# The first u tiles of a hybrid decoder block: 256 tokens multiplied before their norm is known, the rest normalised in turned form

## The chip, the cores and the metric

The kernel runs on one core of a Trainium2 chip. Its metric is the device time of one execution in microseconds (us); lower is better. The engines are named as in the profile: PE is TensorE (products; PEld its weight loads), DVE is VectorE, ACT is ScalarE, POOL is GpSimd, SP is SyncE, which here only issues DMAs. L78 is line 78 of the kernel.

## The reference, cut to what matters

One decoder layer on 512 tokens of width 1024, with 16 meta tokens ahead of them. The start of it, which the change concerns:

```python
def rmsnorm(x, g):
    ms = mean(x * x, axis=-1)
    return x * rsqrt(ms + EPS) * g

h = rmsnorm(concat([meta_tokens, x]), g_mix_pre)      # 528 tokens x 1024
q, k, v, r, a, u, zg, zs = split(h @ w_in)            # 1024 x 6160
```

`a` (16 columns) goes through `w_gate_up` and a log-sigmoid, and its running sums are the decays of a gated linear attention over q, k, v. `u` (1024 columns) goes into S5, a diagonal complex recurrence of 64 groups with coefficients made from `a_re`, `a_im`, `log_step`, `b` and `c`. `zg` and `zs` are the sigmoid gates that merge the two. A squared-ReLU MLP of width 4096 follows. All of it is in float32.

## The kernel before, in words

**Products.** Every float32 operand of a large product is split into a high part (a copy in the rounded type float32r, made by ACT, `split_hi` L159) and a low part (the difference, made by DVE, `split_w_lo` L173). `mm3` (L186) adds three products for each of the 8 slices k of the contraction: high by high, high by low, low by high. So a tile of 128 output columns over 256 tokens is 24 matmuls. The 528 tokens (512 and the 16 meta tokens at the end) are taken in two halves, `HALVES` = 0 to 256 and 256 to 528. Weight tiles of 128 columns (512 KB) have three buffers each for the raw tile, its high and its low part. PSUM has four banks named `mm` and four named `sm`.

**The prologue** (L276 to L428) is in an order written out by hand: `InOrder` (L71) keeps DVE's and ACT's instructions in program order, and `pinned` does it for PE. SP loads the meta tokens, then x in four row tiles of 128 tokens with the first three u weight tiles between them. For each row tile, `squared` sums the squares on ACT, `rooted` makes 1/sqrt with one ACT and four small DVE instructions, `normed` multiplies on DVE by that column and by `gpre` (the gain `g_mix_pre`, spread over the partitions by two products with a row of ones), `turned` transposes eight blocks on PE, and `high` and `low` split the result into `xh` and `xl`. `busy` runs idle products on PE. u tiles 0, 1 and 2 do their first half in between; then come their second halves (L425 to L427), each followed by `u_out`, a store to DRAM issued by POOL. The 16 columns of `a` are split into `wa` (L421 to L423).

**After it** come `gate_weights` (L453), `low_rank` (L458, the product with `wa`), and a list of dense slots. `slot` (L500) first fetches weights for itself and `AHEAD` = 2 more (raw load on SP, high part on ACT, low part on DVE) and then runs the next product of the list: u tiles 3 to 7, four `zs` gates, gate `zg` 4 (L545 to L549). Here the scheduler orders each engine's instructions. Between the slots stand `gate_up` (L473), the S5 coefficients (`chain`, L623, a series of narrow DVE instructions that begins with the tile `ab`, loaded by POOL at L582), their powers, and `decay_sums` (L481): for each of four heads a subtraction and a running sum (`tensor_tensor_scan`) over 528 columns, in which `mask01` sets the sum to zero at each 128th column.

**Blocks.** The rest of the list (L1128 to L1138) is used up as filling for PE in the four heads of attention and the eight S5 blocks (loop at L1145): in each block `slot` is called five times between the pieces of the block. Among the slots are the gates `zg` 5, 6 and 7 (L1133).

Of the kernel before, what the change touches and what calls it, by code (L numbers as in the profile page):

```python
# [9 lines left out]
F32R = mybir.dt.float32r  # L10
# [6 lines left out]
P = 128  # L17
# [32 lines left out]
def hybrid_block(ctx: ExitStack, tc: tile.TileContext, io, out: bass.AP):  # L50
# [66 lines left out]
    S.activation(warm, warm, AF.Sqrt)  # L117
# [137 lines left out]
    def u_half(w, ut, q, within=None):  # L255

        a, b = HALVES[q]
        ps = bank("mm")
        feat_tile(w, xh, xl, a, b, ps[:, : b - a], within=within)

        def taken():
            src = ps.rearrange("p (c s) -> p s c", s=T8)
            first = NM // T8 + a // T8
            S.copy(ut[:, :, first : first + 32], src[:, :, :32])
            if q:
                S.copy(ut[:, :, : NM // T8], src[:, :, 32:34])

        return taken
# [9 lines left out]
    gpre = mk(pxt, [P, D], tag="gpre")  # L278
    grow = mk(pxt, [1, D], tag="grow")
    one_row = mk(pxt, [1, P], tag="one_row")  # L280
    V.memset(one_row, 1.0)
    nc.scalar.dma_start(grow, io["g_mix_pre"][0].rearrange("(o d) -> o d", o=1))
    xm = mk(pxt, [P, D], tag="xt", bufs=5)
    xts, raws = [], []
    loaded = nc.sync.dma_start(xm[:NM], io["meta_tokens"])
    ones = mk(pxt, [P, 256], tag="ones")
    V.memset(ones, 1.0)
    idle = bank()

    def busy(n):  # L290

        for _ in range(n):
            PE.matmul(idle[:, :256], ones[:, :P], ones, start=True, stop=True)
# [3 lines left out]

    def x_load(t):
        xt = mk(pxt, [P, D], tag="xt", bufs=5)
        xts.append((xt, P, t * P))  # L300
        return nc.sync.dma_start(xt, io["x"][0, t * P : (t + 1) * P, :])


    for kind, i in (("x", 0), ("x", 1), ("u", 0), ("x", 2), ("u", 1), ("x", 3), ("u", 2)):
        with behind():
            if kind == "x":
                loaded = x_load(i)
            else:
                loaded, raw = raw_w(w_in[:, C_U + i * P : C_U + (i + 1) * P])
                raws.append(raw)  # L310
    xts.append((xm, NM, SEQ))
# [3 lines left out]
    nc.gpsimd.dma_start(vecs, io["vecs"])  # L315
    V, S = InOrder(nc.vector), InOrder(nc.scalar)
    ss = mk(pxt, [P, 5], tag="xss")
    rs = mk(pxt, [P, 5], tag="xrs")
    xns = {}

    def squared(i):
        xt, n, _ = xts[i]
        sq = mk(pxt, [P, D], tag="xsq", bufs=1)
        S.activation(sq[:n], xt[:n], AF.Square, accum_out=ss[:n, i : i + 1])

    def rooted(i):

        n = xts[i][1]
        y, ssum = rs[:n, i : i + 1], ss[:n, i : i + 1]
        parts = mk(pxt, [n, 2], tag="xr_r", bufs=3)  # L330
        a, hm = parts[:, :1], parts[:, 1:]
        S.activation(a, ssum, AF.Sqrt, scale=1.0 / D, bias=epst[:n])
        yield
        V.tensor_scalar(hm, ssum, -0.5 / D, -0.5 * EPS, op0=ALU.mult, op1=ALU.add)
        V.reciprocal(y, a)
        V.scalar_tensor_tensor(a, y, hm, y, op0=ALU.mult, op1=ALU.mult)
        V.scalar_tensor_tensor(y, a, 1.5, y, op0=ALU.add, op1=ALU.mult)

    roots = {}

    def summed(i):
        squared(i)
        roots[i] = rooted(i)
        next(roots[i])

    def normed(i, cols=(0, 512)):
        xt, n, _ = xts[i]
        if i not in xns:
            xns[i] = mk(pxt, [P, D], tag="xn", bufs=3)
            next(roots[i], None)  # L350
        xn = xns[i]
        for c in cols:
            cc = slice(c, c + 512)
            V.scalar_tensor_tensor(xn[:n, cc], xt[:n, cc], rs[:n, i : i + 1], gpre[:n, cc], op0=ALU.mult, op1=ALU.mult)

    def turned(i, tag):
        return [turned_tokens(xns[i][: xts[i][1]], xts[i][1], q, tag if isinstance(tag, str) else tag[q]) for q in range(2)]

    def high(i, q, pvs):
        _, n, col = xts[i]  # L360
        split_hi(xh[:, 4 * q : 4 * q + 4, col : col + n], pvs[q])

    def low(i, q, pvs):
        _, n, col = xts[i]
        dst = slice(4 * q, 4 * q + 4)
        V.tensor_sub(xl[:, dst, col : col + n], pvs[q], f32(xh)[:, dst, col : col + n])

    gps = [bank() for _ in range(2)]
    for i, ps in enumerate(gps):
        PE.matmul(ps, one_row, grow[:, i * 512 : (i + 1) * 512], start=True, stop=True)  # L370
    busy(2)
    summed(4)
    V.tensor_copy(gpre[:, :512], gps[0])
    normed(4, (0,))
    summed(0)
    S.copy(gpre[:, 512:], gps[1])
    summed(1)
    normed(0)
    t0 = turned(0, "mm")
    busy(2)  # L380
    normed(1)
    hi0 = split_w_hi(raws[0])
    w0 = hi0, split_w_lo(raws[0], hi0)
    high(0, 0, t0)
    high(0, 1, t0)
    t1 = turned(1, "sm")
    high(1, 0, t1)
    high(1, 1, t1)
    for q in range(2):
        low(0, q, t0)  # L390
        low(1, q, t1)
    ut0, ut1, ut2 = (u_tile() for _ in range(3))
    take0 = u_half(w0, ut0, 0)
# [1164 lines left out]
```

## Time and profile before

| | |
|---|---|
| time, median of 3 runs | 884.01 us (882.16 to 884.28) |
| the profiled execution's own time | 883.62 us |
| its span, first to last instruction | 881.9 us |
| mean granted clock of PE | 0.997 |
| DMA | 177.36 MB, mean 201 GB/s |

The span is shorter than the execution's own time by 1.7 us. In the rows of the profile, busy times stand per engine with the number of instructions; "x8" is the number of instructions in a row; an idle time in square brackets names what the instruction had waited for. PE's instructions are pipelined, so a row lasts longer than the distance to the next one.

### The profile page before, as it was taken

The numbers are of one execution on the slowest core, as the hardware profiler recorded it, in microseconds if no ns is written. First come the engines' busy times: TensorE is split into PE (matmuls) and PEld (weight loads), VectorE is DVE, ScalarE is ACT, GpSimd is POOL, SyncE is SP. The second block draws the span as 40 slices with busy tenths as digits, with TensorE's granted clock in tenths as the row PEclk, the third lists the DMA queues.
The fourth block names the chain that finished last, engine by engine and source line by source line (L and its number), as shares of the span: only waits on it lengthen the run. The fifth ranks groups of instructions, "written<-read, shape, count | busy, mean of one in ns | idle before, by whom it ended". The sixth has DMA issues, their size and how long they took to land.

```text
span 881.9 us, 13276 instructions
## 1 busy us (share of the span) xinstructions
PE 869.5 (99%) x4856; PEld 742.5 (84%) x4856; DVE 648.6 (74%) x1148; ACT 437.7 (50%) x731; POOL 124.0 (14%) x224
## 2 busy tenths in 40 slices
PE   8999999999999999999999999999999999999996
PEld 6998989898988888888888888988888888888885
DVE  7989898868778698755445765576666678788886
ACT  6475466767655454434333543333222236665763
POOL 1223022030312213232000001021112100000001
PEclk9999999999999999999999999999999999999998
DMA  9647785555454857558545761589998966856564
GB/s 305 179 126 239 205 196 143 136 134 161 109 166 126 260 130 176 170 161 274 187 143 160 228 178 57 172 288 324 333 305 298 324 244 224 280 190 194 170 209 142
DMA packets 164988, 177.36 MB, mean 201 GB/s; under 512 B 18778, under 2 KB 125306, under 8 KB 164923
## 3 DMA queue, kind: packets, MB, share of 16 engines
q1 hardware_dynamic: 146056, 114.74, 44.8%
q0 software_dynamic: 17696, 57.84, 19.4%
q10 hardware_dynamic: 1170, 3.94, 1.3%
q8 instruction: 38, 0.62, 0.3%
q14 instruction: 28, 0.22, 0.1%
HBM read 141.06 MB, written 35.42 MB: 200 GB/s over the span
## 4 chain that ended last, share of the span: by engine, by line
PE 96%; DVE 2%; ACT 1%; DMA 0%; issue 0%; DVEq 0%; SPq 0%
PE mm L60 73%; PE sm L60 21%; PE sm L65 2%; DMA xt<-in_x_dram 0%; DVE xn L78 0%; DVE wlo L78 0%; ACT xsq L78 0%; DVE c L1483 0%; DVE xl L78 0%; PE mm L65 0%; DVE ede L604 0%; DVE c L1477 0%; ACT xh L78 0%; ACT whi L78 0%; DVEq L1554 0%
## 5 line engine op out<-in xcount | busy, mean ns | idle before, releaser
L160 ACT ACTIVATE whi<-wraw 128x1024 fp32r<-128x1024 f32 x101 | 107.0, 1059 | 236.1 <-PE mm L60 207.9
L175 DVE TENSOR_TENSOR wlo<-wraw,whi 128x1024 fp32r<-128x1024 f32 x101 | 123.4, 1222 | 106.7 <-ACT whi L160 106.5
L60 PE MATMUL mm<-xh,whi 128*128 128x512 f32 (+2 forms) x544 | 182.2, 335 | 0.5 <-ACT xh L78 0.5
L60 PE MATMUL mm<-xl,whi 128*128 128x512 f32 (+2 forms) x544 | 178.6, 328 | 1.1 <-DVE xl L78 1.1
L60 PE MATMUL mm<-xh,wlo 128*128 128x512 f32 (+2 forms) x544 | 178.9, 329 | 0.2 <-DVE wlo L78 0.2
L60 PEld LDWEIGHTS mm<-xh,whi 128*128 128x128 f32 x544 | 102.7, 189 | 10.6 <-issue 1.2
L60 PEld LDWEIGHTS mm<-xl,whi 128*128 128x128 f32 x544 | 102.8, 189 | 10.0 <-DVE xl L78 1.5
L60 PEld LDWEIGHTS mm<-xh,wlo 128*128 128x128 f32 x544 | 102.6, 189 | 9.7 <-DVE wlo L78 0.6
L60 PE MATMUL mm<-hh,whi 128*128 128x512 f32 (+1 forms) x280 | 104.0, 371 | 0.0
L60 PE MATMUL mm<-hl,whi 128*128 128x512 f32 (+1 forms) x280 | 103.8, 371 | 0.0
L60 PE MATMUL mm<-hh,wlo 128*128 128x512 f32 (+1 forms) x280 | 103.8, 371 | 0.0
L1420 DVE TENSOR_TENSOR wlo<-wraw,whi 128x1024 fp32r<-128x1024 f32 x56 | 68.4, 1222 | 20.2 <-ACT whi L1416 20.0
L60 PE MATMUL sm<-wlo,fh 128*128 128x512 f32 x192 | 74.8, 390 | 0.0
L60 PE MATMUL sm<-whi,fl 128*128 128x512 f32 x192 | 74.7, 389 | 0.0
L60 PE MATMUL sm<-whi,fh 128*128 128x512 f32 x192 | 74.7, 389 | 0.0
L1416 ACT ACTIVATE whi<-wraw 128x1024 fp32r<-128x1024 f32 x56 | 58.6, 1048 | 17.2 <-PE mm L60 11.7
L60 PEld LDWEIGHTS mm<-hl,whi 128*128 128x128 f32 x280 | 52.7, 188 | 9.1
L60 PEld LDWEIGHTS mm<-hh,whi 128*128 128x128 f32 x280 | 52.7, 188 | 9.1
L60 PEld LDWEIGHTS mm<-hh,wlo 128*128 128x128 f32 x280 | 52.7, 188 | 8.9
L160 ACT ACTIVATE fh<-f 128x512 fp32r<-128x512 f32 x48 | 30.3, 631 | 45.7 <-PE sm L60 30.6
L60 PE MATMUL mm<-gh,whi 128*128 128x512 f32 x128 | 49.8, 389 | 0.0
L60 PE MATMUL mm<-gl,whi 128*128 128x512 f32 x128 | 49.8, 389 | 0.0
(415 smaller groups left out, 1635.0 us busy)
## 6 DMA issues: line engine op xcount, KB each, us to landing
wraw<-in_w_ff_dram SPq DMA_DIRECT2D x56, 512.0 KB, 4.4
wraw<-in_w_in_dram SPq DMA_DIRECT2D x48, 512.0 KB, 4.1
w2raw<-in_w_ff_dram POOLq DMA_DIRECT2D x16, 1024.0 KB, 8.5
t2d<-w2t POOLq DMA_DIRECT2D x16, 1024.0 KB, 5.8
wraw<-t2d SPq DMA_DIRECT2D x32, 512.0 KB, 3.8
wraw<-in_w_glu_dram SPq DMA_DIRECT2D x16, 512.0 KB, 4.4
M<-kpad POOLq DMA_DIRECT2D x64, 64.0 KB, 2.6
wraw<-in_w_o_gla_dram SPq DMA_DIRECT2D x8, 512.0 KB, 7.9
```

The source lines that it names most:

```text
L60: ins = nc.tensor.matmul(*args, **kw)
L65: ins = nc.tensor.transpose(*args, **kw)
L160: S.activation(dst, src, AF.Copy, scale=scale)
L175: V.tensor_sub(lo, raw, f32(hi))
L1416: halved = S.activation(bh, raw, AF.Copy)
L1420: V.tensor_sub(bl, raw, f32(bh))
```

## The change

The parts, in the order of the program:

1. The input x is given also in turned form (features by tokens), as two arrays `x_cols0` (tokens 0 to 255) and `x_cols1` (256 to 527), and the gain as `g_cols`, one column for each k. These are made where the inputs are laid out, before the launch.
2. SP loads the turned first 256 tokens in four parts of two k; the first u weight tile comes in two halves from ACT's queue. Then SP loads w1, the rows of x 256 to 383, 384 to 511 and of the meta tokens, w2, the turned second half, w3, the rows 0 to 127 and 128 to 255, and w4. The rows are used for their squares alone.
3. For the first 256 tokens of u tiles 0 to 3, the product is made from g·x (`rh`, `rl`) without the per-token scale. The scale comes when the bank is emptied: DVE multiplies by a row that holds each token's 1/sqrt on all partitions (`raw_took`). That row is made by small products with a broadcast column (`spread`).
4. The second half is normalised in turned form (`normed(1)`: for each k one DVE instruction of 272 columns and one ACT copy, and a DVE difference for two k), and its products for tiles 0 to 2 run side by side, k by k.
5. Tile 3's raw product follows, with the squares and roots of rows 0 to 255 and their `spread` in its middle; then `normed(0)`, tile 3's second half, and both halves of tile 4 in the usual way. So five u tiles stand in the prologue, all written in fixed order, and the list of slots begins with u tile 5.
6. The transposes of x, the spreading of the gain and `xn` are gone. The split of `wa` comes at the end, behind the copies of tile 4.
7. The list of early slots has `zg` 4, 5 and 6 where it had `zg` 4, so 5 and 6 leave the later list, and two of the `slot` calls in the last block are left out.
8. `decay_sums` does the difference inside the scan, in five pieces for each head, without `mask01`. `c_rows` and the first fetches are held behind `wa`.

In the order of POOL's instructions, the load of `ab` (third in before) now stands behind the stores of u tiles 0 to 4 and the six loads of `wgu`.

The core of the diff:

```diff
+    def u_took(ps, ut, q, raw=False):
+        a = HALVES[q][0]
+        src = ps.rearrange("p (c s) -> p s c", s=T8)
+        first, n = NM // T8, 32
+        if raw:
+            V.tensor_mul(ut[:, :, first : first + n], src, scale_rows[0])
+            return
+        S.copy(ut[:, :, first + a // T8 : first + a // T8 + n], src[:, :, :n])
+        if q:
+            S.copy(ut[:, :, :first], src[:, :, n : n + first])
...
-    for kind, i in (("x", 0), ("x", 1), ("u", 0), ("x", 2), ("u", 1), ("x", 3), ("u", 2)):
+    for k in (0, 4):
+        first = nc.scalar.dma_start(raws[0][:, k : k + 4], w_in[k * P : (k + 4) * P, C_U : C_U + P].rearrange("(k p) n -> p k n", p=P))
+    for k in range(0, KT, 2):
+        with behind():
+            loaded = nc.sync.dma_start(xT[:, k : k + 2, :256], io["x_cols0"][:, k : k + 2])
...
+    for kind, i in (("u", 1), ("x", 2), ("x", 3), ("x", 4), ("u", 2), ("h", 0), ("h", 4), ("u", 3), ("x", 0), ("x", 1), ("u", 4)):
...
+    def taken_raw(k):
+        g = g8[:, k : k + 1]
+        S.activation(rh[:, k], xT[:, k, :256], AF.Copy, scale=g)
+        V.scalar_tensor_tensor(rl[:, k], xT[:, k, :256], g, f32(rh)[:, k], op0=ALU.mult, op1=ALU.subtract)
...
+    def spread(c, cols):
+        ps = bank()
+        for j, i in enumerate(range(c.start, c.stop)):
+            n = xts[i][1]
+            PE.matmul(ps[:, j * P : j * P + n], rs[:n, i : i + 1].to_broadcast([n, P]), ident[:n, :n], start=True, stop=True)
+        return ps[:, : cols.stop - cols.start]
...
+        def scaled(k):
+            V.scalar_tensor_tensor(xT[:, k, cols], xT[:, k, cols], g8[:, k : k + 1], rows[:, cols], op0=ALU.mult, op1=ALU.mult)
+            S.copy(xh[:, k, cols], xT[:, k, cols])
+        def rest(k):
+            kk = slice(k, k + 2)
+            V.tensor_sub(xl[:, kk, cols], xT[:, kk, cols], f32(xh)[:, kk, cols])
...
+    busy(5)
...
+    for k in range(0, KT, 2):
+        for i in range(2):
+            taken_raw(k + i)
+        split_part(w0, raws[0], slice(k, k + 2))
+    pair = bank("mm")
+    raw_product(0, w0, pair)
+    for k in (0, 4):
+        split_part(w1, raws[1], slice(k, k + 4))
+    raw_product(1, w1, pair)
+    for i in range(2, TT + 1):
         squared(i)
+    rooted(late)
+    w2_ = split_w(raws[2])
+    ps = spread(late, lasts)
+    S.copy(rows[:, lasts], ps)
+    pair2 = bank("mm")
+    raw_product(2, w2_, pair2)
+    normed(1)
+    seconds = [bank("mm"), bank("mm"), bank()]
+    c0, c1 = HALVES[1]
+    for k in range(KT):
+        for (hi, lo), ps in zip((w0, w1, w2_), seconds):
+            for i, (a, b) in enumerate(((hi, xh), (hi, xl), (lo, xh))):
+                PE.matmul(ps[:, : c1 - c0], a[:, k], b[:, k, c0:c1], start=(k == 0 and i == 0), stop=(k == KT - 1 and i == 2))
+    w3 = split_w(raws[3])
+    squared(0)
+    squared(1)
+    rooted(early)
...
+    raw_product(3, w3, pair2, within=(4, spread_early))
+    for i in range(3):
+        u_took(seconds[i], uts[i], 1)
+    for i in range(2):
+        raw_took(i, pair)
+        u_out(i, uts[i])
+    w4 = split_w(raws[4])
     normed(0)
+    raw_took(2, pair2)
+    u_out(2, uts[2])
+    uts.append(u_tile())
+    raw_took(3, pair2)
+    u_half(w3, uts[3], 1)
+    u_out(3, uts[3])
+    uts.append(u_tile())
+    for q in range(2):
+        u_half(w4, uts[4], q)
+    u_out(4, uts[4])
     wa = mk(pg, [P, KT, 32], F32R, tag="wa")
-    split_hi(wa[:, :, :16], wraw)
+    begun_s = S.activation(wa[:, :, :16], wraw, AF.Copy)
...
-            V.tensor_sub(mn[:, h], mn[:, h], ga[:, h])
             b2 = mk(pga, [P, NT], tag="b2", bufs=2)
-            V.tensor_tensor_scan(b2, mask01, mn[:, h], 0.0, op0=ALU.mult, op1=ALU.add)
+            for c in range(0, NT, P):
+                cc = slice(c, min(c + P, NT))
+                V.tensor_tensor_scan(b2[:, cc], mn[:, h, cc], ga[:, h, cc], 0.0, op0=ALU.add, op1=ALU.subtract)
...
-    for m in range(3, KT):
+    for m in range(5, KT):
         u_slot(m)
...
-    gate_slot(C_ZG, 4, zg, early_tile)
+    for m in range(4, 7):
+        gate_slot(C_ZG, m, zg, early_tile)
...
-        slot()
+        if b < NBLK - 1:
+            slot()
```

More of the change, by code (lines that the diff above doesn't have):

```diff
@@ L321, in squared @@
     def squared(i):
[L322 to L334, printed above, removed]
+        xt, n = xts[i]
@@ L356, in turned @@
[L356 to L370, printed above, removed]
@@ L412, in hybrid_block @@
-    t3 = turned(3, ("mm", "sm"))
-    take1()
-    for q in range(2):
-        high(4, q, t4)
-        low(4, q, t4)
-    for q in range(2):
-        high(3, q, t3)
-        low(3, q, t3)
-    take2()
+    def spread(c, cols):
[4 more added lines that the diff above has]
+        return ps[:, : cols.stop - cols.start]
@@ new lines, in hybrid_block, with split_part @@
+    w1 = tuple(mk(wp, [P, KT, P], F32R, tag=t, bufs=3) for t in ("whi", "wlo"))
+    def split_part(w, raw, kk):
+        split_hi(w[0][:, kk], raw[:, kk])
+        V.tensor_sub(w[1][:, kk], raw[:, kk], f32(w[0])[:, kk])
+    for k in range(0, KT, 2):
+        for i in range(2):
[6 more added lines that the diff above has]
+    raw_product(1, w1, pair)
@@ L1188, in hybrid_block @@
         next(following, None)
-        slot()
+        if b < NBLK - 1:
+            slot()
         if this:
```

163 lines of the change are left out of this document (66 added, 97 removed).

## The prediction

> **What bounds the kernel now.** I read the page first: its span, its busy shares and the chain that ended last.
>
> ```profile
> span 881.9 us, 13276 instructions
> ...
> PE 869.5 (99%) x4856; PEld 742.5 (84%) x4856; DVE 648.6 (74%) x1148; ACT 437.7 (50%) x731; POOL 124.0 (14%) x224
> ...
> PE 96%; DVE 2%; ACT 1%; DMA 0%; issue 0%; DVEq 0%; SPq 0%
> ```
>
> TensorE is busy 869.5 of 881.9 us, so at most 12.4 us can come from removing its waits. Next come the waits of TensorE.
>
> ```profile
> PE sm L60 <- DMA grow<-in_g_mix_pre_dram: 2.6, 1, 2.6
> PE mm L60 <- DVE xl L78: 1.1, 2, 0.7
> ```
>
> Both belong to the prologue (with three more rows of 0.5 us and less, they are all that the view lists). So I took the chain of waits of the first 60 us, and the windows.
>
> ```profile
> 1.26 4.25 DMA xt<-in_x_dram
> ...
> 27.71 18.86 PE mm L60 x151
> ```
>
> ```profile
> 0.00:28.00 28.00, 23.36 (x127) 18.06 (x128) 21.97 (x65) 19.49 (x37) 7.53 (x25) 1.00 0.93 292
> 28.00:40.00 12.00, 12.00 (x99) 11.52 (x99) 11.02 (x56) 4.97 (x11) 2.21 (x4) 1.00 0.50 140
> 40.00:60.00 20.00, 20.00 (x166) 19.91 (x165) 19.74 (x71) 12.46 (x27) 3.94 (x6) 1.00 0.51 131
> 60.00:80.00 20.00, 20.00 (x132) 18.41 (x131) 16.55 (x32) 14.47 (x25) 4.39 (x8) 1.00 0.61 197
> 80.00:100.00 20.00, 20.00 (x97) 16.88 (x96) 19.20 (x30) 8.09 (x12) 3.99 (x7) 1.00 0.82 241
> ```
>
> Columns: length, then busy time of PE, weight load, DVE, ACT, POOL. Two things carry the forecast. From 27.71 on TensorE never stops: 151 products in 18.86 us are 0.125 us each, 72 of them make the three second halves. And DVE is nearly as full in 28 to 100 (66.5 of 72 us), with only a little time before TensorE asks for its results.
>
> **The change, part one: the prologue.** My yardstick is the start L of the low-rank product, which stands behind the u tiles.
>
> ```profile
> 13.60 0.38 PE L60 MATMUL mm<-xh,whi 128*128 128x256 f32 x1 [0.25 <-ACT xh L78]
> ...
> 36.70 0.28 PE L60 MATMUL mm<-xh,wa 128*32 128x256 f32 x1
> ```
>
> In before L is 36.70 with three u tiles. The change has five there. One tile is 24×0.120 + 24×0.125 = 5.88 us, which before does later at full pace, so equal cost would be L = 36.70 + 2×5.88 = 48.46.
>
> The durations that I use:
>
> ```profile
> 5.53 1.06 ACT L78 ACTIVATE xsq<-xt 128x1024 f32<-128x1024 f32 x1 [1.15 <-DMA xt<-in_x_dram]
> 6.49 0.19 ACT L78 ACTIVATION_READ_ACCUMULATOR xsq<-xt 128x1 f32 x1
> 6.71 0.29 ACT L78 ACTIVATE xr_r<-xss,epst 128x1 f32<-128x1 f32 x1
> ...
> 8.76 1.04 ACT L78 ACTIVATE whi<-wraw 128x1024 fp32r<-128x1024 f32 x1
> ...
> 27.15 0.33 ACT L78 ACTIVATE wa<-waraw 128x128 fp32r<-128x128 f32 x1
> ```
>
> ```profile
> 7.69 1.41 DVE L78 SCALAR_TENSOR_TENSOR xn<-xt,xrs,gpre 128x512 f32<-128x512 f32 x2
> ...
> 19.66 1.22 DVE L78 TENSOR_TENSOR wlo<-wraw,whi 128x1024 fp32r<-128x1024 f32 x1
> ...
> 31.61 0.19 DVE L586 TENSOR_SCALAR eme<-emr 128x64 f32<-128x64 f32 x1
> 31.72 0.19 DVE L586 TENSOR_SCALAR emk<-emk 128x64 int32<-128x64 f32 x1
> ...
> 50.84 1.69 DVE L479 TENSOR_SCALAR mn<-sm,vecs 128x256 f32<-128x256 f32 x4
> 52.45 0.41 DVE L224 TENSOR_TENSOR lp4a<-lamp 128x256 f32<-128x256 f32 x1
> ...
> 67.83 0.71 DVE L485 TENSOR_TENSOR mn<-mn,ga 128x528 f32<-128x528 f32 x1 [1.30 <-ACT ga L483]
> ...
> 68.73 1.25 DVE L487 TENSOR_TENSOR_SCAN b<-mask,mn 128x528 f32<-128x528 f32 x1
> ```
>
> A DVE instruction starts some 0.07 to 0.08 us before the one ahead of it ends (0.19 long, 0.11 apart), so I charge 1.13 for 1024 columns, 0.65 for a normalising 512, 0.34 for 256. A normalising instruction of 256 or 272 columns, which before lacks, lies between 0.34 (the plain 256) and 0.65 (512); I take 0.40, near the lower row. A tile of squares with its sum costs 1.18 (5.53 to 6.71), a root 0.3, a high part 0.95 to 1.04.
>
> Up to 15.6 us. DVE makes the raw parts of the first tile in four groups of 2×0.40+0.34, 4.6 us, and TensorE follows it to about 9.6; the second raw tile ends near 13. That beats before, whose first product runs at 13.6. But then nothing can go on until the squares of x rows 256 to 511 and the meta tokens are summed. Ahead of and with these rows 3.21 MB are asked for (w0 0.52, turned x 1.05, w1 0.52, rows 1.11). How fast they come, in slices of 1.25 us of the first 50:
>
> ```profile
> GB/s 0 69 203 380 365 361 406 340 415 352 292 365 364 321 311 312 325 325 346 350 251 61 69 10 0 0 47 224 278 327 173 247 225 102 290 41 0 0 0 0
> ```
>
> The first nine slices hold 3.17 MB by 11.25 us. The first issue is now 0.4 us sooner, and in before x0 (0.58 MB with the meta tokens, crossed by 4.4) counted as landed at 5.51, 1.1 later: 12.0 us, between 10.9 (no such lag) and 13 (0.3 MB of other tiles mixed in). Then two squares to 14.4, the root 0.3, four small DVE operations 0.9: **15.6**. TensorE idles 2.6 us.
>
> 15.6 to 28.6. The weights of tile 2 are split behind the root (high 15.7, low 16.95), so raw 2 ends at 19.6. The 72 interleaved second halves take 9.0 us; normalising for them (8×0.41 + 4×0.6 = 5.8 us of DVE) runs ahead of them. The 40 transposes are gone; in before they stood in TensorE's gaps.
>
> 28.6 to L. Tile 3's weights take over tile 0's buffers, which the interleaving holds to its last k: high 27.9 to 28.95, low to 30.2, a stall of about 1.4. The squares of x0 and x1 stand behind that split on ACT (31.3), root and DVE to 32.4, the spreading product sits in the middle of raw 3 and waits another 1.0: raw 3 ends at 34.35, tile 3's second half at 37.35. DVE has the low part of w4 till 37.1 and then normalises the first 256 tokens, 8×0.40 + 4×0.6 = 5.5, to 42.6: tile 4's first half ends at 43.3 (stall 3.0), its second at 46.3. The split of `wa` now stands behind tile 4's last copies on ACT: some 0.5 for these, 0.33 and 0.28 for the two parts, with nothing else for TensorE: 47.4. The same bookkeeping over before's prologue gives 27.3 where the row says 27.71; I add that 0.4: **L = 47.8, a gain of 0.7** against 48.46 (bounds: 46.7 and 48.9 by the landing alone). So the early start is paid back by stalls at other places: 2.6, 1.4, 1.0, 3.0 and 1.1.
>
> **Part two: what the prologue now pushes back.** The S5 coefficients begin with `ab`. In before POOL issues its load third, at 2.95. In the changed order it stands on POOL behind the stores of tiles 0 to 4 and six `wgu` loads, and its store of tile 4 waits for that tile.
>
> ```profile
> 2.95 0.56 POOL L582 DMA_DIRECT2D ab<-in_a_step_dram  x1
> ...
> 25.98 1.94 POOL L449 DMA_DIRECT2D wgu<-in_w_gate_up_dram  x4
> ```
>
> ```profile
> wgu<-in_w_gate_up_dram POOLq DMA_DIRECT2D x6, 32.0 KB, 2.0
> ab<-in_a_step_dram POOLq DMA_DIRECT2D x1, 96.0 KB, 5.3
> ```
>
> Tile 4 is copied by 46.9; its store, four of the loads and `ab` itself, at 0.5 to 0.6 of issue each, make 50; landing 2.0 to 5.3 us after, with some waiting for the queue: **52 to 56, I take 54.5**, near the row of `ab` itself. From there DVE has, ahead of the low part of the ninth slot's weights (zg 5): 103 operations of 64 columns at 0.11 to 0.16 (15.0), 8 of 1024 (9.0), 10 of 512 (6.0), 20 of 128 and 256 (5.1), 20 pieces of scan (5.6; in before four scans of 1.17 and four differences of 0.63, 7.2), 8 gate rows of 0.41 (3.3), 1 for the rest: 45 us, so 99.5 (97 to 101). TensorE wants those weights at about 98.3 if nothing stopped it. **A new wait of 0 to 3 us, I take 1.2.** Behind this wlo on DVE stands the rest of the tables of block 0, and TensorE's only other need of them is this:
>
> ```profile
> 91.57 0.69 DVE L995 TENSOR_TENSOR M<-M,B 128x512 f32<-128x512 f32 x1
> ```
>
> ```profile
> 104.10 0.67 PE L60 MATMUL sm<-M,BA 128*32 128x128 f32 x16
> ```
>
> Before is 11.8 us early there; the change puts two gate slots (zg 5 and 6, 11.8 us) ahead of that product, and the tables end at 106 to 110 against a need at 115: no wait. Gate products 2 and 3 take banks that DVE empties in the same full stretch, 0.5 us.
>
> **Part three.** Two slots leave the last block, so TensorE's filling there is 11.8 us shorter and its tables come some 6 us ahead of use instead of 18: still ahead, cost nothing (4 us if they come 10 us later than I read). The turned copies of x are made before the launch, and 26 KB less of broadcast loads cost nothing, as SP's queue is not what ends.
>
> **Sum.** −0.7 + 0.5 + 1.2 = +1.0 on the profiled execution's 883.62 us (span 881.9 and 1.7 around it): 884.6. The median of the runs shown is 884.01, 0.4 above that execution, so this is less than 0.1% from it. A measurement of this kernel tells about 0.3%, 2.65 us, from no change: 881.4 to 886.7 counts as the same.
>
> **A rule that speaks to the start.**
>
> ```profile
> 10.31 1.91 PE L60 MATMUL sm<-ones 128*128 128x256 f32 x4
> ```
>
> ```profile
> 132.42 1.46 PE L60 MATMUL sm<-vtok,ktok 128*128 128x256 f32 x6
> ```
>
> The same records of 256 columns take 0.48 us at 10.3 and 0.24 at 132, though the granted clock reads 1.00 in both: early products run at half pace until about 12 us. Here that is hidden (raw 0 at 24×0.24 from 6 to 11.8, raw 1 after it at full pace to 14.8, still before 15.6). The Trainium skill, "TensorE: Matmul & The Clock Gate", Part 1, says that the clock starts at half and is released after about 3.4 us of sustained activity, and falls back after an idle window of the same length. The trace differs on the first half: nine microseconds after TensorE began it is still slow. The page's fall-back would make an idle stretch like the 2.6 us one costly if it grew to 3.4: some 1.7 us by the page's figure, an estimate.
>
> **The rivals.**
>
> *Sooner rows* (0.26): the rows land at 10.9 and the normalising instructions of 272 columns are as cheap as plain ones. Then L is 1.1 + 0.4 sooner, the 0.4 of my bookkeeping falls too, `ab` follows, and part two costs 0.5 at most or nothing: −0.7−1.5−0.4 = −2.6, 881.0. For it: GB/s in the early slices reached 415, and turned x comes in pieces of 1 KB. Against: before's own first tile was 1.1 late.
>
> *DVE backlog* (0.20), the other side: `ab` lands at 56 or later, DVE gets the 45 us done at 101 or later, and TensorE waits 3 to 4 us for the ninth slot, 887.4 with the 0.5. It decides from a landing at about 55.5. For it: DVE is 99% and 96% full at 40 to 60 and 80 to 100 even with an early start. Against: 1.6 us less scan work.
>
> *Clock* (0.06): TensorE falls back to half pace in the wait before 15.6 and stays there as long as at the start, 9.4 us with the work of 4.7: 889.3.
>
> *It does not do what it says* (0.04): the last block starves without its two slots, 4 us, 888.6; or tile 4 waits for DVE as long as the transposes did.
>
> **How the numbers follow.** The forecast has the remaining 0.44, between 882.5 and 886.3. Faster by over 0.3%: three quarters of the first rival and a small part of the forecast's lower end, 0.23. Slower: 0.15 of the second, the third and fourth, and 0.02 of the forecast, 0.27. The same: 0.50. The range must hold 8 in 10: it takes in the sooner rows with its own spread, 880.5, and the backlog to 888.0; beyond are the clock, half of the last and the tails.
>
> **What would show it.** A row of squares of x3 that starts near 12.0 (10.9 for the first rival); a spreading product at 15.6; waits of TensorE on `wlo` near 29 (1.4) and on `xl` near 40 (3.0); low-rank product at 47.8; the first operation on `ab` at 54.5; a wait on `wlo` of 1.2 near 98, and none on the M product. It is wrong if L is outside 46 to 49, or if a wait over 2 us stands at a place that I have not named.

## The result, and the profile after

The changed kernel takes 888.33 us (median of 5 runs, 887.17 to 890.96), the kernel before 882.68 us in the same comparison (5 runs, 882.03 to 884.28). The ratio is 1.0065, with a 95% interval from 1.0043 to 1.0087: **slower by 5.65 us**, where the forecast had +1.0 and a range that ended at 888.0. The profiled execution of after took 889.77 us, its span 887.8, 5.9 longer than before's 881.9.

The page of after, the rows that answer to those of before:

```profile
span 887.8 us, 13258 instructions
...
PE 866.4 (98%) x4824; PEld 740.9 (83%) x4824; DVE 648.4 (73%) x1169; ACT 438.9 (49%) x742; POOL 124.4 (14%) x220
...
PE 87%; DVE 6%; DMA 3%; ACT 2%; issue 1%; SPq 0%; DVEq 0%; ACTq 0%
```

TensorE has 3.1 us less to do (866.4 after 869.5) and yet the span is 5.9 longer, so 9 us of waiting are new. The chain that ended last says the same: 87% of it runs over TensorE, where it was 96%. The waits of TensorE in after (total, times, longest):

```profile
PE sm L60 <- DVE xrs L78: 2.6, 2, 2.1
PE sm L65 <- DVE e_gk L901: 2.2, 1, 2.2
PE mm L60 <- ACT whi L78: 2.0, 2, 1.7
PE mm L60 <- DVE xl L78: 1.8, 3, 1.0
PE mm L60 <- DVE wlo L174: 1.5, 1, 1.5
PE sm L60 <- DVE xss L328: 1.3, 1, 1.3
PE mm L60 <- DVE wa L78: 1.2, 1, 1.2
PE mm L60 <- DVE wlo L78: 0.8, 1, 0.8
PE mm L60 <- ACT xh L78: 0.4, 1, 0.4
```

The rows with L78 (and `xss`, at the very start) are the prologue, and most of them were forecast. Two stand behind it: `wlo` of L174, which was forecast, and `e_gk` of L901, which was not. Where they stand in time, with the start L of the low-rank product and the M product (timeline of TensorE):

```profile
16.80 1.00 PE L60 MATMUL sm<-ident,xrs 128*128 128x128 f32 x6 [2.12 <-DVE xrs L78]
...
50.43 0.28 PE L60 MATMUL mm<-xh,wa 128*32 128x256 f32 x1 [1.16 <-DVE wa L78]
...
102.22 0.50 PE L60 MATMUL mm<-xh,wlo 128*128 128x512 f32 x1 [1.50 <-DVE wlo L174]
...
118.78 0.66 PE L60 MATMUL sm<-M,BA 128*32 128x128 f32 x16
...
141.94 0.62 PE L65 MATMUL sm<-ident,e_gk 128*16 128x128 f32 x4 [2.18 <-DVE e_gk L901]
...
418.20 0.39 PE L60 MATMUL mm<-gh,whi 128*128 128x512 f32 x1
```

The answering rows of before, the last two of them in TensorE's timeline:

```profile
125.10 0.60 PE L65 MATMUL sm<-ident,e_gk 128*16 128x128 f32 x4
...
412.23 0.39 PE L60 MATMUL mm<-gh,whi 128*128 128x512 f32 x1
```

The last row is the first product of the GLU, behind all the u tiles and gates. There after is 5.97 late, and it is 5.9 late at the end; TensorE has no wait on record in between: **everything is lost by 142 us**, and the last blocks cost nothing. The loss is at three places. L stands at 50.43 against 48.46 for equal cost: 2.0. The waits at 102 and at 142 are 1.5 and 2.2. That is 5.7 of 5.97. This is the account of one execution, which at 889.77 us is 1.4 above the median.

### The profile page after: what moved, and what is told of

Same layout as the page of the kernel before. It is cut to its first block, busy times and chain, and to the rows that moved or that the text cites. A ratio compares the mean times of both kernels' runs of the same rounds, so it can differ in the third digit from the quotient of the medians.

```text
span 887.8 us, 13258 instructions
## 1 busy us (share of the span) xinstructions
PE 866.4 (98%) x4824; PEld 740.9 (83%) x4824; DVE 648.4 (73%) x1169; ACT 438.9 (49%) x742; POOL 124.4 (14%) x220
## 3 DMA queue, kind: packets, MB, share of 16 engines
q1 hardware_dynamic: 147448, 116.90, 45.7%
## 4 chain that ended last, share of the span: by engine, by line
PE 87%; DVE 6%; DMA 3%; ACT 2%; issue 1%; SPq 0%; DVEq 0%; ACTq 0%
PE mm L60 64%; PE sm L60 21%; PE sm L65 2%; DMA wraw<-in_w_in_dram 1%; DVE wlo L174 1%; DMA xt<-in_x_dram 1%; DVE b L512 1%; ACT xt L78 0%; DMA g<-in_g_cols_dram 0%; DVE xT L78 0%; SPq L1034 0%; DVE mta L234 0%; DVE epb L235 0%; DVE M L1012 0%; DVE c L1512 0%
## 5 line engine op out<-in xcount | busy, mean ns | idle before, releaser
L159 ACT ACTIVATE whi<-wraw 128x1024 fp32r<-128x1024 f32 x99 | 104.6, 1059 | 231.1 <-PE mm L60 200.2
L174 DVE TENSOR_TENSOR wlo<-wraw,whi 128x1024 fp32r<-128x1024 f32 x99 | 120.9, 1223 | 106.0 <-ACT whi L159 105.9
L60 PE MATMUL mm<-xh,whi 128*128 128x512 f32 (+2 forms) x504 | 170.5, 338 | 0.4 <-ACT xh L78 0.4
L60 PE MATMUL mm<-xl,whi 128*128 128x512 f32 (+2 forms) x504 | 167.4, 332 | 1.8 <-DVE xl L78 1.8
L60 PE MATMUL mm<-xh,wlo 128*128 128x512 f32 (+2 forms) x504 | 167.5, 332 | 1.5 <-DVE wlo L174 1.5
L60 PEld LDWEIGHTS mm<-xl,whi 128*128 128x128 f32 x504 | 95.2, 189 | 10.9 <-DVE xl L78 2.4
L60 PEld LDWEIGHTS mm<-xh,wlo 128*128 128x128 f32 x504 | 95.0, 189 | 11.0 <-DVE wlo L174 1.9
L60 PEld LDWEIGHTS mm<-xh,whi 128*128 128x128 f32 x504 | 95.1, 189 | 10.2 <-issue 1.0
L1449 DVE TENSOR_TENSOR wlo<-wraw,whi 128x1024 fp32r<-128x1024 f32 x56 | 68.4, 1223 | 20.7 <-ACT whi L1445 20.7
L1445 ACT ACTIVATE whi<-wraw 128x1024 fp32r<-128x1024 f32 x56 | 58.7, 1049 | 18.3 <-PE mm L60 11.7
```

Source lines behind the costliest of these rows:

```text
L60: ins = nc.tensor.matmul(*args, **kw)
L159: S.activation(dst, src, AF.Copy, scale=scale)
L174: V.tensor_sub(lo, raw, f32(hi))
L1445: halved = S.activation(bh, raw, AF.Copy)
L1449: V.tensor_sub(bl, raw, f32(bh))
```

## The experiments

My theory from these rows: (a) in the prologue the x rows land late, TensorE idles, its clock falls, and L is late; (b) the load of `ab` stands so late on POOL that VectorE carries its table work behind it up to 142 us, and TensorE waits for VectorE twice. The rivals were that the clock alone explains the prologue, that the new scans explain VectorE's lateness, and that TensorE's waits on VectorE would come anyway.

### The tables: earlier in the new kernel, later in the old one

**e1_ab_early**: the new kernel with the load of `ab` at its old place.

```diff
     nc.gpsimd.dma_start(vecs, io["vecs"])
+    ab = mk(p5, [P, 3, NST_N], tag="ab")
+    nc.gpsimd.dma_start(ab, io["a_step"])
...
-    ab = mk(q5, [P, 3, N], tag="ab")
-    nc.gpsimd.dma_start(ab, io["a_step"])
```

> The changed kernel, with the tile ab in a pool that exists before the prologue and its load issued right behind that of vecs, so that the S5 chain on DVE can begin behind the last eviction of tile 3 (about 46 us) and not at 56.5. Theory (DVE backlog): the waits of TensorE of 1.5 us at 102 and of 2.2 us at 142 both come from DVE's late start; both go, and the time falls from 888.3 by 3.0 to 3.9 us, to about 884.6. Rival (SP queue): the wait at 142 comes from the loads of the block's states, which stand behind weight loads on SP; then only the 1.5 goes, to about 886.8. Second rival (the waits belong to the moved slots): nothing changes, 888.

Measured: 890.27 us, ratio 1.0085 (1.007 to 1.01). No gain. TensorE's timeline has no wait at `e_gk` any more, but these:

```profile
51.90 0.39 PE L60 MATMUL mm<-xh,wa 128*32 128x256 f32 x1 [2.49 <-DVE wa L78]
...
99.86 0.50 PE L60 MATMUL mm<-xh,wlo 128*128 128x512 f32 x1 [1.72 <-DVE wlo L174]
...
142.65 0.60 PE L65 MATMUL sm<-ident,e_gk 128*16 128x128 f32 x4
```

With `ab` there, the scheduler puts the table steps ahead of the split of `wa` on VectorE. The wait at `wa` grows from 1.16 to 2.49, and the one on `wlo` stays (1.72): here the order that VectorE gets counted, and not the landing of `ab`. Behind the longer wait the granted clock is at 0.50 as well (window of 52 to 54 us). That the wait at `e_gk` is gone doesn't show that it hangs on the tables: VectorE has `e_gk` ready at 140.28, 1.6 sooner than in after (141.89), but TensorE comes to it 2.9 later (142.65, where after asked at 139.76). In e16 below, without this edit, it is ready at 139.82. So (b) is not shown by e1, and an earlier load doesn't repair the time.

**e4_before_ab_late**: the reverse. The kernel before, with that load held behind the last copy of the low-rank product.

```diff
             S.copy(alow[r0:r1, a:b], ps[:32])
+        S.copy(ab[:32, 0, :1], f32(alow)[:32, NT - 1 :])
+        nc.gpsimd.dma_start(ab, io["a_step"])
...
-    nc.gpsimd.dma_start(ab, io["a_step"])
```

> The kernel before, with one edit: the load of ab waits for the last copy of the low-rank product (about 44 us), so that the S5 chain on DVE begins near 48 us, 11 us behind the start of the low-rank product (in the changed kernel 6 us behind it). Theory (DVE backlog): it alone makes the kernel before slower, 4 to 9 us, with waits of TensorE on DVE (low parts of weights, or the M product at 104) where it has none now. Rival: DVE makes the time good within its 11.8 us of slack, and the time stays within 1 us of 882.7.

Measured: 895.6 us, ratio 1.0141 (1.0124 to 1.0158), 12.7 us lost with nothing else changed. Its timeline of TensorE, and a window of it (length, busy time of PE, weight load, DVE, ACT, POOL, granted clock):

```profile
108.43 0.58 PE L60 MATMUL mm<-xh,wlo 128*128 128x256 f32 x1 [9.79 <-DVE wlo L175]
```

```profile
108.00:114.00 6.00, 5.57 (x28) 5.57 (x29) 6.00 (x11) 0.53 (x2) 0.00 (x0) 0.57 0.38 103
```

One wait of 9.79, and then a granted clock of 0.57 on average for 6 us. Late tables alone can cost far more than the whole change does.

**e5_chain_in_gap**: `ab` early, and the first three of the table steps in the fixed order, right behind the normalising of the second half.

```diff
     normed(1)
+    for _ in range(3):
+        next(steps)
     seconds = [bank("mm"), bank("mm"), bank()]
```

> The changed kernel, with the load of ab early and the first three steps of the S5 chain (47 narrow DVE instructions, about 6 us) written into the prologue's fixed order behind the second normalisation, where DVE idles from 24.2 to 31.8 us. Theory (DVE backlog by amount of work): the low-rank product still starts near 50.4 (not at 51.9 as with the early load alone, which put chain instructions ahead of the split of wa), and TensorE's waits on DVE near 102 (1.5) and 142 (2.2) both go: about 884.6. Rival (place in the queue): the low part of the ninth slot's weights waits because the scheduler puts table work ahead of it on DVE, however much has been done before; then 1.5 to 1.7 us stay near 100, and the time is about 886.2.

Measured: 890.98 us, ratio 1.009 (1.0075 to 1.0105). Both late waits are gone, and one has come in the prologue, on the low part of u tile 3's weights, which stands behind the steps:

```profile
37.17 0.58 PE L60 MATMUL mm<-rh,wlo 128*128 128x256 f32 x1 [4.84 <-DVE wlo L78]
```

L goes to 56.16, 5.7 later than in after. That is more than the two late waits together (3.7), so they would be gone by TensorE's own lateness, whatever the tables do. And `e_gk` is ready at 141.77, against 141.89 in after: with the steps done early it is no sooner. So e5 doesn't show (b) either. What it shows is that this place in the prologue does not hold the steps for nothing.

### The clock

**e2_fill** puts five idle products behind the second raw tile; **e3_both** is this together with e1; **e15_fill_both** has the five and three more at the start. **e16_after_again** is the changed kernel once more, in the same comparison as e15.

```diff
     raw_product(1, w1, pair)
+    idle = bank()
+    busy(5)
```

> The changed kernel, with five more idle products on TensorE behind the second raw tile, so that it does not idle between 14.7 and 16.8 us. Theory (clock): the granted clock of 0.50 between 18 and 21.5 us follows from that idle stretch; with it filled the clock stays at 1.00, raw tile 2 takes 2.9 us and not 4.6, the low-rank product starts about 1.5 us sooner (48.9) and the time falls by about 1.5, to 886.8. Rival (the low clock comes from something else, such as the way the first 20 us are loaded): the clock falls all the same, and the time stays at 888.3 or rises by what the idle products delay.

> Both edits, the early load of ab and the five idle products. If the two causes are separate, the gains add: 888.3 - 3.7 - 1.5 = 883.1, which is about the kernel before (882.7). If the 1.5 us at the start are given back as a longer wait later, it is the same as the early load alone, about 884.6.

> The changed kernel with eight idle products at the start instead of five, and five behind the second raw tile. Theory (clock): neither half-clock stretch (8 to 11 and 18 to 21.5 us) is left, the low-rank product starts 1.5 to 2 us sooner than in the changed kernel run beside it, and the median is lower by 1 to 2. Rival (what the start gains, the waits on DVE near 100 and 142 take back): the median is the same within 0.7.

> The changed kernel again, unaltered, beside the two others: 888.3, between 887 and 891 in single executions.

Measured: e2 888.81 (1.0066, 1.0051 to 1.0081), e3 888.55 (1.0069, 1.0046 to 1.0092), e15 888.58 (1.0065, 1.0052 to 1.0077), e16 889.51 (1.0079, 1.0064 to 1.0093). The windows of after show what the filling was for. The first two are stretches of 2 us, the last three stretches of 3.41 us:

```profile
19.00:21.00 2.00, 2.00 (x11) 2.00 (x11) 2.00 (x6) 1.46 (x4) 0.00 (x0) 0.50 1.02 401
21.00:23.00 2.00, 2.00 (x17) 2.00 (x16) 2.00 (x6) 1.29 (x4) 0.00 (x0) 0.87 1.23 290
```

```profile
4.38:7.79 3.41, 1.68 (x8) 1.01 (x7) 1.69 (x5) 2.16 (x6) 0.00 (x0) 1.00 1.04 332
14.62:18.03 3.41, 1.29 (x9) 1.11 (x8) 2.02 (x6) 2.34 (x5) 0.00 (x0) 1.00 1.12 370
31.68:35.09 3.41, 2.03 (x13) 1.63 (x13) 2.05 (x6) 2.44 (x6) 0.00 (x0) 1.00 0.20 45
```

The granted clock is 0.50 at 19 to 21; the products of raw 2 then follow one another at 0.21 us instead of 0.12. The half clock lasts from 18.1 to 21.5 and costs raw 2 about 1.5 us; an earlier stretch is at 7.9 to 11.3. In the 3.41 us ahead of them TensorE was busy for 1.68 and 1.29; the third stretch (2.03) has no fall behind it. That is no sharp limit: in e16, e7 and e2 a fall came behind 1.87, 1.94 and 2.22 of 3.41.

In e2 the fall at 18 is absent (one at 9.3 is there) and L is 49.45, a gain of 1.0 in the trace. But the median of e2 is that of after. The second execution of after, e16, helps to see why. Its timeline of TensorE, and that of e15 behind it:

```profile
49.05 0.27 PE L60 MATMUL mm<-xh,wa 128*32 128x256 f32 x1 [1.16 <-DVE wa L78]
...
100.85 0.50 PE L60 MATMUL mm<-xh,wlo 128*128 128x512 f32 x1 [1.50 <-DVE wlo L174]
...
139.88 0.62 PE L65 MATMUL sm<-ident,e_gk 128*16 128x128 f32 x4 [1.51 <-DVE e_gk L901]
```

```profile
49.05 0.28 PE L60 MATMUL mm<-xh,wa 128*32 128x256 f32 x1 [1.16 <-DVE wa L78]
...
101.78 0.50 PE L60 MATMUL mm<-xh,wlo 128*128 128x512 f32 x1 [2.44 <-DVE wlo L174]
...
139.84 0.62 PE L65 MATMUL sm<-ident,e_gk 128*16 128x128 f32 x4 [0.50 <-DVE e_gk L903]
```

e16 is the same program as after, with the clock at half from 9.4 to 12.8 and not at 18: the fall depends on the execution, and L is 1.4 sooner without the one at 18 (49.05 against 50.43). e15 has no half clock at all and no earlier L than e16. And the two waits behind L are together 2.94 in e15 and 3.01 in e16; VectorE has `e_gk` ready at 139.8 in both. So what TensorE gained at the first wait it lost at the second.

How much of the 5.65 can be the clock? The granted clock of each execution is on record. Of the ten executions of the changed kernel (after and e16) the three with 0.996 or 0.997 take 887.2 to 888.6 us, the three with 0.991 take 890.6 to 891.0. So the clock goes with some 3 us between one execution and the next, but those with the highest clock are still 4.5 to 5.8 above the kernel before. And e7, below, has both falls in its profiled execution (at 8.5 and 18.7) and nevertheless the time of before. So the clock adds to single executions and is not the cause of most of the 5.65.

### The rows

**e7_rows_early** loads x rows 0 and 1 ahead of u tile 3's weights, so that their squares, root and spreading run during the interleaved second halves. With this the order of the work changes as well: the spreading stands inside those products, and the first half is normalised in two parts, one on each side of the split of tile 3's weights.

```diff
-    for kind, i in (("u", 1), ("x", 2), ("x", 3), ("x", 4), ("u", 2), ("h", 0), ("h", 4), ("u", 3), ("x", 0), ("x", 1), ("u", 4)):
+    for kind, i in (("u", 1), ("x", 2), ("x", 3), ("x", 4), ("u", 2), ("h", 0), ("h", 4), ("x", 0), ("x", 1), ("u", 3), ("u", 4)):
...
+        if k == 5:
+            spread_early()
...
+    normed(0, 0, 4)
+    w3 = split_w(raws[3])
+    normed(0, 4)
+    raw_product(3, w3, pair2)
```

> The changed kernel, with the rows of x 0 to 255 loaded ahead of w3, their squares, roots and spreading product during the interleaved second halves, and half of the first half's normalisation ahead of the low part of w3, the other half right behind it. DVE and ACT idle there (24 to 31). TensorE's waits between 31 and 45 us (3.8 in all: 0.3, 0.8, 0.5, 0.4, 1.0, 0.4, 0.4) should shrink to about 1, and the low-rank product start near 47.5 instead of 50.4. If TensorE's later waits on DVE keep their size: 885.4. If DVE's backlog takes it back (the chain starts no earlier in the same degree): 887 to 888.

Measured: 882.64 us (10 runs, 881.15 to 885.64), ratio 0.9996 (0.9986 to 1.0006): all of the loss is gone. TensorE's timeline:

```profile
46.31 0.28 PE L60 MATMUL mm<-xh,wa 128*32 128x256 f32 x1 [1.16 <-DVE wa L78]
...
97.80 0.50 PE L60 MATMUL mm<-xh,wlo 128*128 128x512 f32 x1 [1.19 <-DVE wlo L174]
...
135.15 0.60 PE L65 MATMUL sm<-ident,e_gk 128*16 128x128 f32 x4
...
411.40 0.39 PE L60 MATMUL mm<-gh,whi 128*128 128x512 f32 x1
```

L is 4.1 sooner than in after, the `e_gk` wait is gone, and the end is 6.8 sooner (span 881.0). The stalls at the spreading of the first rows and at tile 4 do not stand in its list of waits. `ab` is used first at 51.9, 4.6 sooner. VectorE has `e_gk` ready at 134.51, 7.4 sooner than in after, and TensorE asks for it 4.6 sooner. So the order of the prologue sets both parts of the loss: the late L and the waits behind it. Which of the three changes of e7 does how much is not shown, nor is the way by which they reach `e_gk`; that it goes through the place of `ab` behind tile 4's store is argued only.

**e6_wa_early** moves the split of `wa` ahead of tile 4's products.

```diff
     u_out(3, uts[3])
+    wa = mk(pg, [P, KT, 32], F32R, tag="wa")
+    begun_s = S.activation(wa[:, :, :16], wraw, AF.Copy)
+    begun = V.tensor_sub(wa[:, :, 16:], wraw, f32(wa)[:, :, :16])
     uts.append(u_tile())
```

> The changed kernel, with the split of wa ahead of tile 4's product in the fixed order instead of behind its last copies. The forecast's term of 1.1 us (1.2 in the trace of the changed kernel) goes, the low-rank product starts at 49.2: 887.1. Rival: DVE's later waits take it back, since the rest of DVE's work is no earlier: 888.3.

Measured: 890.07 us, ratio 1.0081 (1.0064 to 1.0097). The wait of 1.16 is gone and L is 48.02 in its trace, but the gate products now wait for the banks that VectorE empties (0.70 and 0.97 near 66), `wlo` 1.49 near 102, `e_gk` 0.98. Against e16, which lacks the edit, L is 1.0 sooner and these waits are together 1.1 longer: the gain of TensorE ahead of a late VectorE is handed on as a wait.

### The scans

**e11_scan_back** is the new kernel with before's subtraction and masked scan; **e13_before_scan** is the kernel before with the new pieces.

```diff
-            V.tensor_sub(mn[:, h], mn[:, h], ga[:, h])
-            V.tensor_tensor_scan(b2, mask01, mn[:, h], 0.0, op0=ALU.mult, op1=ALU.add)
+            for c in range(0, NT, P):
+                cc = slice(c, min(c + P, NT))
+                V.tensor_tensor_scan(b2[:, cc], mn[:, h, cc], ga[:, h, cc], 0.0, op0=ALU.add, op1=ALU.subtract)
```

> The changed kernel with the running sums of the kernel before (four differences, four scans of 528 columns with the mask). DVE has about 1.6 us more work by the durations of the kernel before. Theory (backlog by amount): TensorE's waits on DVE near 102 and 142 grow by about as much in all, 1 to 1.6 us: 889.5. Rival (the waits come from the place in the queue, not from the amount): no change, 888.3.

> The kernel before with the changed running sums alone (20 pieces, no differences). DVE has some 1.6 us less work at 68 to 82 us, where TensorE waits for nothing: no change, 882.9 to 883.3. Rival (a shorter DVE queue is worth time even here): 1 us faster.

Measured: e11 896.84 (1.016, 1.0146 to 1.0174); e13 886.14 (1.0034, 1.0022 to 1.0046). In e11 the old scans bring not 1.6 but 8.5 us over after. The 1.6 of work can't be the reason alone. VectorE's timeline, and below it TensorE's:

```profile
114.93 1.22 DVE L790 TENSOR_TENSOR M<-M,prm 128x1024 f32<-128x1024 f32 x1 [6.62 <-DMA M<-in_b_cols_dram]
```

```profile
148.15 1.02 PE L65 MATMUL sm<-ident,e_gk 128*16 128x128 f32 x4 [3.65 <-DVE e_gk L904]
```

With the other scans VectorE got another order. In it an instruction that needs a DMA stands 6.62 us at the head of the queue, with two low parts of weights behind it, and TensorE waits 0.84, 2.53 and 3.65, which is 3.3 more than in after. Most of the rest is the clock: it falls to 0.50 for two stretches of 3.4 us from 120.3 on and for one from 147.7 on, beside the two early ones that after has too, and each costs up to 1.7 us. e13's own profiled execution (884.07) has waits of only 0.32, 0.39 and 0.24 near 87, 98 and 108 beyond those of before. That explains some 0.5 to 1 of its 3.26 us, and the rest stays open: the profiled execution is the fastest of five. So the rival of the scans is not excluded: by themselves the new pieces cost the kernel before 3.26. But e7 has them too and takes before's time, so they are no fixed price.

### Versions that put the repairs together

**e8_all**: rows early, `wa` early, `ab` early, five idle products, and a table step in each of two gaps of the fixed order. **e9_rows_wa_ab**: the same without the steps in the gaps. **e14_chain_w3_first**: as e8, with tile 3's weights split before any normalising of the first half, and without the second of the two steps. **e17_chain_held**: as e8, with the later steps held behind `wa`. The core of the edits, beside those of e6 and e7:

```diff
     for k in (0, 4):
         split_part(w1, raws[1], slice(k, k + 4))
+    next(steps)
     raw_product(1, w1, pair)
...
-        next(steps, None)
+        with tc.issue_after(begun.ins):
+            next(steps, None)
```

> All edits on the changed kernel: five idle products behind the second raw tile, the chain's first step (17 instructions) where DVE waits for the squares and more of it behind the second normalisation, the rows of x early with the normalisation split, and wa split ahead of tile 4. If the causes add up: 888.3 - 2.9 - 1.2 - 1.5 - 3.7 = 879.0, faster than the kernel before by 3.9. If TensorE again runs ahead of DVE's table work (the waits near 100 and 142 come back because the low-rank product is 5 us sooner): 882 to 884.

> On the changed kernel: the rows of x 0 to 255 early with the normalisation split (as in the run that did this alone), the five idle products, the split of wa ahead of tile 4, and the early load of ab, whose chain can now no longer stand ahead of wa. If the prologue's causes add up and DVE's earlier chain keeps pace: the low-rank product at 43.5 to 44, no wait at 142, at most 1.5 near 98, so 882.6 - 1.2 - 1 = about 880.5, faster than the kernel before by 2 to 3. Rival (TensorE sooner means only a longer wait on DVE near 98): 882 to 883, the same as the kernel before.

> As the run with all edits (idle products, rows of x early, wa ahead of tile 4, the S5 chain begun in DVE's idle time), but with the split of w3 ahead of the normalisation of the first 256 tokens, so that ACT doesn't have it behind copies that wait for DVE. If the causes add up: the low-rank product near 45 (48.65 there), no wait on DVE near 100 or 142, 880 to 881.5, faster than the kernel before by 1.5 to 3. Rival: the time saved at the start comes back as a wait on DVE near 95, 883.

> The kernel with all the edits of e8_all, but the later steps of the table chain are held on VectorE until wa's half is done, so that only the first two steps stand in gaps of the prologue. Theory (the tables start late, and each wait is set by what stands ahead of them on VectorE): the equal-cost start of the low-rank pass falls to about 44 to 46 (it was 44.18 in e9 and 48.65 in e8), there is no wait of over 0.3 on wlo near 95 and none at the exponentials, and the time is 880 to 882, 1 to 3 below before. Rival (the steps that are held are missed again later): a wait of 1.5 to 2 on VectorE near 92 to 95 comes back, and the time is 882.5 to 884, the same as before.

Measured: e8 884.05 (1.001, 1.0001 to 1.002), e9 884.54 (1.0017, 1.0006 to 1.0027), e14 884.64 (1.0018, 1.0009 to 1.0027), e17 885.98 (1.0041, 1.0028 to 1.0055). None beats the kernel before or e7. In e9 L falls to 44.18, 4.3 below equal cost, and TensorE then waits 1.91 for `wlo` at 92.3. Of the 2.1 us by which it is ahead of e7 at L, 1.3 are gone at the gate products near 61 and the rest at this wait. In e8 and e17 ACT splits tile 3's weights behind four high parts that wait for VectorE, and the wait at that place grows (0.28 in after, 2.75 in e8). TensorE's timeline of e17, and two of its windows of 3.41 us:

```profile
33.56 0.39 PE L60 MATMUL mm<-rh,whi 128*128 128x256 f32 x1 [2.28 <-ACT whi L78]
```

```profile
32.46:35.87 3.41, 1.56 (x10) 1.35 (x11) 3.18 (x6) 1.73 (x4) 0.00 (x0) 1.00 0.26 77
35.87:39.28 3.41, 3.41 (x18) 3.41 (x17) 2.81 (x7) 2.91 (x10) 0.82 (x2) 0.50 0.58 152
```

A wait of 2.28, a stretch with 1.56 busy, and then 3.41 us at a clock of 0.50. The time falls out of one place and comes back at another.

## Why the prediction was wrong, point by point

The sum was +1.0 where the trace has +5.9. Of the steps:

- **The first raw tiles**: "raw 1 after it at full pace to 14.8". It ended at 14.7, but by another path, so this is partly luck: raw 0 began at 7.0 and not at 6, had two products 0.12 apart at 7.7 (full pace), and then ran through a fall of the granted clock (7.9 to 11.3) that was not in the working. The main text had put the end at 13.
- **The rows**: "12.0 us, between 10.9 (no such lag) and 13". The squares of x3 began later, on ACT's timeline of after:

```profile
13.34 1.06 ACT L78 ACTIVATE xt<-xt 128x1024 f32<-128x1024 f32 x1 [0.64 <-DMA xt<-in_x_dram]
...
30.68 1.06 ACT L78 ACTIVATE whi<-wraw 128x1024 fp32r<-128x1024 f32 x1 [7.30 <-PE mm L60]
```

  This is 1.3 late and outside the bounds that I gave. The whole chain shifted by 1.2 (spreading product at 16.80, not 15.6).
- **The clock**: the sum had nothing for it. I gave it a chance of 0.06, as 9.4 us of half pace, and thought the idle time costly only "if it grew to 3.4". It fell behind 2.1 us, for 3.4 us, and cost 1.5 in this execution. My reading that products run at half pace until about 12 us failed too: at 7.7 they are at full pace. Whether the idle products at the start of before were at half pace stays open, as the granted clock reads 1.00 there.
- **From there to L** the working held in its sum: 19.75 us from the high part of tile 3's weights (30.68) to L (50.43), forecast 19.9. Its stalls were 1.0, 0.5, 2.2 and 1.2 for 1.4, 1.0, 3.0 and 1.1. They are 1.6 less, so the rest was about as much more, which I can't place: two misses cancelled. L was 2.6 late, 50.43 for 47.8, by the two terms ahead of this stretch.
- **`ab`**: used first 6.7 behind L in the forecast, 6.1 in the trace (56.53), POOL issuing it here:

```profile
52.54 0.57 POOL L608 DMA_DIRECT2D ab<-in_a_step_dram  x1
```

- **The wait for the ninth slot's weights**: 1.2 near 98; measured 1.50 at 102.22. Right. The 0.5 for gate products 2 and 3 did not come.
- **The two gate slots**: 11.8 us is the price of two u tiles. A gate is 24 products of 512 columns, 0.23 apart in the trace, so two are 10.9. That moves the need at M by 0.9, and no term of the sum.
- **"TensorE's only other need of them is this", the M product: the step that failed.** There was no wait at M, as said. But the next product that needs VectorE is the one of `e_gk`, and this I had not looked at. VectorE's timeline of before, and of after behind it:

```profile
123.53 0.70 DVE L874 TENSOR_TENSOR e_gk<-kT,e_gk 128x528 f32<-128x528 f32 x1
```

```profile
115.56 0.68 DVE L1023 TENSOR_TENSOR M<-M,B 128x512 f32<-128x512 f32 x1
...
141.19 0.70 DVE L901 TENSOR_TENSOR e_gk<-kT,e_gk 128x528 f32<-128x528 f32 x1
```

  In before it is ready at 124.23 for a product at 125.10: 0.9 us of slack, behind 11.8 at M. In after M is ready 2.5 ahead of its product (116.24 for 118.78, forecast 5 to 9 ahead), and `e_gk` comes 2.2 after TensorE asked. Slack at one need said nothing of the next. Nor is `e_gk` late behind one unbroken queue of tables. From the first use of `ab` to the wait at 102 VectorE is busy for 45.0 of 45.7 us, but then it idles twice, for high parts of weights from ACT:

```profile
113.82 1.23 DVE L174 TENSOR_TENSOR wlo<-wraw,whi 128x1024 fp32r<-128x1024 f32 x1 [2.56 <-ACT whi L159]
...
131.52 1.23 DVE L174 TENSOR_TENSOR wlo<-wraw,whi 128x1024 fp32r<-128x1024 f32 x1 [1.90 <-ACT whi L159]
```

  ACT had waited 10.4 us for a load of weights ahead of the first of these. What makes `e_gk` late is therefore open: the table backlog (b) is borne out for the wait at 102 at most. In the chain that ended last, that load and one of `U` (2.1 us, at 132) stand on the way to `e_gk`, so loads are a rival, and no run tried it.
- **The last block**: cost nothing, as forecast; the shift is 5.97 at 418 and 5.9 at the end.

Put together: +1.0 forecast, +2.6 at L, +0.3 at the ninth slot, +2.2 at `e_gk`, −0.5 at the gates make 5.6 of 5.9; 0.3 is not placed. So three terms failed: the landing of the rows (1.2), the clock, which was put at nothing (1.5), and the need at `e_gk`, which was put at nothing (2.2). That the order of the prologue is the root is shown by e7, which moves the first rows and the work that hangs on them and has before's time. That late tables cost time by themselves is shown by e4; that the two waits of after hang on them is not shown, neither by e1 nor by e5. That filling against the clock helps the median is not shown: e2 and e15, whose profiled executions lack the second fall, are at 888.6 to 888.8, after at 888.3 and 889.5. Of the rivals, the backlog of VectorE and the clock both came, each in part; I had given them 0.26 together as if only one could happen.

Three things stay open: what makes `e_gk` late; how much of the spread of 2 to 4 us between the runs of one kernel is the clock (in e13 the two don't go together); and whether an arrangement with rows early and steps in the gaps can be clearly below before, which four attempts were not.

## What to carry to other kernels

When work is moved ahead of a table or a load, list every later product that takes something from the delayed engine, with its slack in the trace, not only the one that asked last; the smallest slack counts. Ask of every gain on the engine that sets the end whether the engine that feeds it can follow: here 1 us won ahead of a late VectorE came back as a wait (e6, e9). And ahead of a prologue in a fixed order, price the landing of each load with its bytes in front: here one pair of loads one place further forward, with the work that hangs on it, was worth 5.7 us (e7). And when a wait disappears, see whether the awaited result came sooner or the waiting engine came later (e1, e5).

## What the runs showed of the hardware

The granted clock fell to 0.50 for stretches of 3.4 us. In the 3.41 us ahead of a fall TensorE was busy for 1.68 and 1.29 (after), 1.56 (e17), 1.87 (e16), 1.94 (e7) and 2.22 (e2); behind 2.03 in after it did not fall, so busy time by this view gives no sharp limit. The longest unbroken wait ahead of a fall was 1.7 and 2.1 us in after and 1.5 in e16; a wait of 1.4 later in e16 had no fall behind it. The same program had its falls at 7.9 and 18.1 in one execution and at 9.4 alone in another. The Trainium skill, "TensorE: Matmul & The Clock Gate", Part 1, describes a free-running window of 3413 ns whose phase differs by run; the trace agrees with this, with stretches of 3.4 us. The same part has the clock fall after at least one idle window of about 3.4 us; here the measurement differs, as the clock fell behind windows in which TensorE was busy for 1.3 to 2.2 us.

A short VectorE instruction took nearly five times as long as its neighbours while POOL worked. In e1's timeline of VectorE five instructions of 64 columns, of which four take 0.23 and one 1.09, last 2.67 together, while POOL runs a selection over 512 columns and issues DMAs. The cause of that was not tried.

```profile
47.17 2.67 DVE L630 SCALAR_TENSOR_TENSOR ede<-ede,edr 128x64 f32<-128x64 f32 x5
```
